# The modulation sums of two k-tiles move from TensorE to VectorE

## The chip, the cores and the metric

The kernel runs on one core of one Trainium2 chip. The metric is the device time of one execution in microseconds (us). The kernel before takes 2005.23 us, the median of three runs (2004.79 to 2006.36). Traces come from the hardware profiler, which records one execution.

## The reference, cut to what matters

One trunk layer of a diffusion backbone works on 384 tokens of width 2048: 128 context tokens and 256 latent ones. All arithmetic is fp32.

```
m = silu(cond) @ w_mod + b_mod        # (2048) @ (2048, 6*2048), once per condition
sh1, sc1, g1, sh2, sc2, g2 = split(m, 6)
h = rms_norm(x, n1) * (1 + sc1) + sh1 # context tokens take c_ctx's row, latent ones c's
p = h @ w_in                          # (384, 2048) @ (2048, 4096): q, k, v, u
... attention, Fourier mixing, gates, output projection, SwiGLU FFN
```

The change touches how `sh1` and `sc1` of norm 1 are made: two matrix-vector products over 2048 rows and 2 x 2048 columns, for two conditions. Each 128 of the 2048 channels of `h` are one k-tile of the product with `w_in`. A k-tile of `h` can be made only when its shift and scale columns are there.

## The kernel before, in words

**Large products.** A weight is kept as a high and a low half in a reduced fp32 form, and so is `h`; each product is three matmuls (lines 170, 171 and 176: high-high, low-high, high-low). Work is cut into units: two k-tiles of weights by 512 columns (one k-tile where a group's count is odd), for the three tiles of 128 tokens. `next_unit` goes ahead of each unit. It has the next unit's weights split (`split`, line 155 on ScalarE for the high half, line 156 on VectorE for the low half), then ticks every side job in `behind`, and asks SyncE for one more load of weights. There are four raw buffers and three for each half.

**Groups.** The product with `w_in` has eight chunks of 512 columns (`ORDER`). It doesn't run chunk by chunk over all 16 k-tiles, since these come one after another. It runs in `GROUPS`: k-tile 0 for all chunks, then k-tiles 1 and 2, then 3 to 6, then 7 to 15. That makes 8 units in the second group, 16 in the third, and 40 in the last. After a chunk in a group, VectorE adds the PSUM tiles to the chunk's sum in SBUF (line 783). In the second and third group the PSUM tiles come from the pool `mm` with four buffers, three to a chunk.

**Norm 1's modulation.** `MODS` lists the k-tiles whose sums are made together as (first, count). `mod_sums` (lines 427 to 446) runs 8 steps for each entry: two k-rows of `w_mod`, shift and scale, four matmuls that use four column groups of the array side by side (line 436), each `count` x 128 columns wide. The weights come in tiles `wm` with four buffers, loaded by SyncE (line 419), two k-rows at a time (four where the count is one). When a step has used up a tile, the next load is asked for. After the last step ScalarE copies the sums (line 444). `mod_cols` turns them by TensorE transposes, one per k-tile (line 452), and VectorE adds the biases (lines 458 to 460). `modulate` makes a k-tile of `h`: ScalarE lines 553 and 155, VectorE line 156.

**The order.** All of this is written out by hand. `prepare` is a generator which yields after each step: a step of sums, with a step of the k-tiles before it as follower. `Paced` runs a generator at a rate: every unit adds `rate` to what is due, and when at least `least` is due, whole steps are run until less than one is left. `DUE` and `PREP` give the start and the rate in each group; in the last two groups `least` is 3.6, so that steps come in bursts. Thirteen steps are issued by hand in the opening. A unit whose k-tiles are not there forces steps (line 779).

**What follows.** When `prepare` ends, `with_rows` gives back the memory of `wm` and starts `rows`: the sums of the other four modulations. Those are made on VectorE (lines 361 and 363), from loads of 512 KB, summed over partitions by accumulating transfers on GpSimd's queue, and paced by `CHUNKS` in the last group. Before, counted from the rates, `prepare` ends in the fourth unit of the last group.

Of the kernel before, what the change touches and what calls it, by code (L numbers as in the profile page):

```python
# [13 lines left out]
F32 = mybir.dt.float32  # L14
F32R = mybir.dt.float32r
AF = mybir.ActivationFunctionType
ALU = mybir.AluOpType
AX = mybir.AxisListType

P = 128  # L20
D = 2048
KT = D // P
# [10 lines left out]
CH = 512  # L33
# [2 lines left out]
HALF = NL + NC  # L36


MODS = [(0, 1), (1, 2), (3, 2), (5, 2), (7, 3), (10, 3), (13, 3)]
GROUPS = [(0, 1), (1, 2), (3, 4), (7, 9)]  # L40
ORDER = [6, 7, 0, 1, 2, 3, 4, 5]
DUE = [-1.4, 0, 0, 0]
PREP = [1.75, 2.5, 1.8, 1.8]
PAIR = "t1 qk,,,,,lq,s0 s1 m0,e0,m1,i0 pv lb,e1,,i1 t0,,lv"


# [73 lines left out]
def trunk_kernel(ctx: ExitStack, tc: tile.TileContext, io: dict):  # L120
    nc = tc.nc
# [21 lines left out]
    dram = ctx.enter_context(tc.tile_pool(name="dram", bufs=1, space=DRAM))  # L143
# [90 lines left out]
    front, behind = [], []  # L234
# [25 lines left out]
    ident = consts.tile([P, P], F32, tag="ident", name="ident")  # L260
    make_identity(nc, ident)
    ones = consts.tile([P, 32], F32, tag="ones", name="ones")
    nc.vector.memset(ones, 1.0)
    csz = consts.tile([P, KT, 32], F32, tag="csz", name="csz")
# [8 lines left out]
    def new_h(kt):  # L273
# [16 lines left out]
    conds, ng, bcol = (first[:, 32 * i : 32 * i + 32] for i in range(3))  # L290
    ng = ng.rearrange("p (i k) -> p i k", i=2)
# [3 lines left out]
    ms1 = consts.tile([P, KT, 2, 2], F32, tag="ms1", name="ms1")  # L295
    msh, msc = (
        [ms1[:, :, i], consts.tile([P, KT, 2], F32, tag=f"ms2{i}", name=f"ms2{i}")] for i in range(2)
    )
# [8 lines left out]
    with ExitStack() as ph:  # L307
# [159 lines left out]
        with ExitStack() as pha:  # L467
            wmp = phm.enter_context(tc.tile_pool(name="wmp", bufs=4, side="right"))
            cpool = pha.enter_context(tc.tile_pool(name="cpool", bufs=12))
            tmp = pha.enter_context(tc.tile_pool(name="tmpa", bufs=2))  # L470
# [24 lines left out]
            def head_constants():  # L495
                nc.sync.dma_start(heads, io["heads"])
                yield
                yield
                yield
                nc.vector.tensor_scalar_mul(qg8, qg[:, 0:1], HD**-0.5)  # L500
# [42 lines left out]
            scales = Paced(scale())  # L543
# [12 lines left out]
            for t in range(NT):  # L556
                for cc in range(4):
                    turn(t, cc, acc_tile)
                    square(t, cc)
                    if t == 0 and cc == 2:  # L560
                        nc.scalar.activation(
                            out=csz[:, :, 0:2], in_=conds.rearrange("p (k c) -> p k c", c=2), func=AF.Silu
# [17 lines left out]
            prepared = [1]  # L580
# [13 lines left out]
            def prepare():  # L594

                follow = iter(())
                for k0, n in MODS[1:]:
                    for i, _ in enumerate(mod_sums(src, k0, n, wme, sums)):
                        if i:
                            next(follow, None)  # L600
                        yield
                    follow = columns_and_tokens(k0, n)
                    if k0 + n == KT:
                        prep.due = min(prep.due, 0)
                        yield
                    while k0 + n in (3, 7) and prepared[0] < k0 + n:
                        prep.due = min(prep.due, 0)
                        yield
                        while prepared[0] < k0 + n:
                            yield next(follow)  # L610
                for _ in follow:
                    yield

            prep = Paced(prepare())

            h0H, h0L = new_h(0)
            f0 = tmp.tile([P, TOK], F32, tag="hf", name="hf0")
# [110 lines left out]
                rpool = phr.enter_context(tc.tile_pool(name="rpool", bufs=1, side="right"))  # L728
                behind.append(rows)

            prep.then = with_rows
            behind += [scales, prep]

            def after(ci):
                a = acc[ci]
# [30 lines left out]
            for gi, (k0, n) in list(enumerate(GROUPS))[1:]:  # L766
                prep.due, prep.rate = DUE[gi], PREP[gi]
                prep.least = 3.6 if gi > 1 else 1
                if gi == len(GROUPS) - 1:
                    behind.append(Paced(head_constants(), 0.2))  # L770
                    new_ring()
                for rate, ci in zip(CHUNKS, ORDER):
                    if gi == len(GROUPS) - 1:
                        rows.rate = rate
                    po = [(mm_tile if gi < len(GROUPS) - 1 else acc_tile)() for _ in range(NT)]
                    for u in range(k0, k0 + n, 2):
                        w = next_unit()
                        while prepared[0] < min(u + 2, k0 + n):
                            prep.step()

                        def done(t):
                            a = acc[ci][:, t]
                            nc.vector.tensor_add(a, a, po[t])  # L783

                        unit(po, hH, hL, w, u, min(k0 + n - u, 2), u == k0, u + 2 >= k0 + n, done)
                    if gi == len(GROUPS) - 1:
                        behind.append(Paced(after(ci)))
# [407 lines left out]
    tmp = ctx.enter_context(tc.tile_pool(name="tmpx", bufs=2))  # L1195
# [207 lines left out]
    parts = [([], []) for _ in FF_PARTS]  # L1403
# [147 lines left out]
def _laid_out(inp):  # L1551


    def by_chunk(w):
        k, n = w.shape
        return w.reshape(k // P, P, n // CH, CH).transpose(2, 1, 0, 3)

    def columns(v):
        return v.reshape(-1, P).T

    out = _tables()
    for name in ("w_in", "w_na_proj", "w_fnet_proj", "w_gate", "w_o", "w_gate_up", "w_down"):
        out[name] = by_chunk(inp[name][0])
    x = np.concatenate([inp["x_prompt"][0], inp["x_sample"][0]], axis=0)
    out["x_in"] = x.reshape(NT, P, 4, CH).transpose(2, 1, 0, 3)

    w_mod, b_mod = inp["w_mod"][0], inp["b_mod"][0]
    shift_scale = w_mod[:, : 2 * D].reshape(KT, P, 2, D).transpose(1, 0, 2, 3)
    for kt0, n in MODS:
        out[f"w_mod{kt0}"] = shift_scale[..., kt0 * P : (kt0 + n) * P]  # L1570
    out["w_rows"] = w_mod[:, 2 * D :]
    out["b_mod"] = b_mod
    conds = np.stack([columns(inp["c_ctx"]), columns(inp["c"][0])], axis=2).reshape(P, -1)
    out["first"] = np.concatenate(
        [conds, columns(inp["norm1_g"][0]), columns(inp["norm2_g"][0]), columns(b_mod[: 2 * D])], axis=1
    )
    qg, kg = inp["q_norm_g"][0], inp["k_norm_g"][0]
    out["heads"] = np.concatenate(
        [np.tile(qg, 2)[:, None], np.tile(kg, 2)[:, None], np.tile(kg, (P, 1))], axis=1
    )  # L1580

    cache_k = inp["cache_k"][0, 0].reshape(P, NH // 2, P)
    out["cache_k"] = cache_k.transpose(1, 2, 0)
    out["cache_v"] = inp["cache_v"]

    q, c = np.arange(HD)[:, None], np.arange(HD)[None, :]
    h, rr, e = np.arange(NH), np.arange(2), np.arange(6)
    at = (
        h.reshape(8, 1, 1, 2, 1, 1) * 465
        + (5 + e.reshape(1, 1, 1, 1, 6, 1) - rr.reshape(1, 2, 1, 1, 1, 1)) * 31  # L1590
        + (15 + np.clip(c - q, -15, 15)).reshape(1, 1, HD, 1, 1, HD)
    )
    w0 = np.clip(q - 8, 0, 48)
    inside = ((c >= w0) & (c < w0 + 16)).reshape(1, 1, HD, 1, 1, HD)
    places = np.append(inp["rpb"][0].reshape(-1), np.float32(-1e30))
    out["rpb"] = places[np.where(inside, at, len(places) - 1)].reshape(8, P, 2, 6, HD)
    return {n: np.ascontiguousarray(a) for n, a in out.items()}
# [27 lines left out]
```

## Time and profile before

| what | value |
|---|---|
| median of three runs | 2005.23 us |
| the profiled execution | 2005.29 us |
| its span, first to last instruction | 2003.5 us |
| TensorE busy | 1989.5 us (99%) |
| VectorE busy | 1226.0 us (61%) |
| ScalarE busy | 718.3 us (36%) |
| GpSimd busy | 73.9 us (4%) |
| line 436, the sums on TensorE | 448 records, 13.4 to 168.9 us |
| granted TensorE clock | 1.0 throughout |

In the rows of the profile PE is TensorE, PEld its weight loads, DVE VectorE, ACT ScalarE, POOL GpSimd, SP SyncE. A group row gives line, engine and operation, output and inputs, count, then busy time and mean ns of one, then the engine's idle time just before them and what ended it. A timeline row gives start and duration in us; a duration of several instructions run together is from the first start to the last end. In brackets stands the idle time before, and who ended it. A matmul of fp32 data leaves two records, a transpose one. Ends of matmuls are modelled, and some records are missing.

### The profile page before, as it was taken

Reading aid. Unit: us, or ns where it says so; the run is one execution under the profiler, and the core shown is the slowest. Engines: PE = TensorE matmul, PEld = TensorE weight load, DVE = VectorE, ACT = ScalarE, POOL = GpSimd, SP = SyncE. Lnnn points to the kernel's source line nnn. Section 1 sums busy time; section 2 is a strip of 40 time slices with the busy share of each in tenths; the row PEclk is TensorE's granted clock in tenths of the full one; section 3 lists DMA queues with packets and bytes.
Section 4 is the critical chain, followed back from the end, with each engine's and each line's share of the span. In section 5 each row is a group of like instructions: output and inputs, shape, how many; then the busy total and the mean of one; then the engine's idle time right before and its main releaser. Section 6 shows DMA issues by size and latency. Waiting matters only on the chain.

```text
span 2003.5 us, 24190 instructions
## 1 busy us (share of the span) xinstructions
PE 1989.5 (99%) x9404; PEld 1628.4 (81%) x9404; DVE 1226.0 (61%) x1493; ACT 718.3 (36%) x1052; POOL 73.9 (4%) x106
## 2 busy tenths in 40 slices
PE   8999999999999999999999999999999999999999
PEld 5767888887777888889988888888888888888887
DVE  6745999879877886776843454554334433434654
ACT  6324332445554443344423322323232233223231
POOL 0000010101010100100001000001000000000000
PEclk9999999999999999999999999999999999999999
DMA  9896898888886898764457464547444544455463
GB/s 347 289 342 206 308 288 312 271 278 283 269 255 216 284 330 264 252 231 131 134 182 200 158 189 164 188 139 211 137 150 129 165 153 131 132 152 174 158 185 104
DMA packets 140658, 425.28 MB, mean 212 GB/s; under 512 B 17856, under 2 KB 39296, under 8 KB 139520
## 3 DMA queue, kind: packets, MB, share of 16 engines
q1 hardware_dynamic: 127344, 400.51, 60.4%
q0 software_dynamic: 9600, 16.88, 3.9%
q10 hardware_dynamic: 3600, 6.34, 0.9%
q8 instruction: 74, 1.21, 0.2%
q14 instruction: 40, 0.33, 0.0%
HBM read 387.50 MB, written 44.63 MB: 216 GB/s over the span
## 4 chain that ended last, share of the span: by engine, by line
PE 95%; DMA 2%; DVE 2%; ACT 1%; issue 1%; SPq 0%; DVEq 0%; ACTq 0%
PE mm L170 19%; PE mm L176 18%; PE mm L171 18%; PE at L170 10%; PE at L171 10%; PE at L176 10%; PE at L436 1%; DMA wm<-in_w_mod 1%; PE at L1039 1%; PE at L977 1%; PE at L1056 1%; DVE wl L156 1%; PE at L1447 1%; PE at L1453 1%; PE mm L1453 1%; PE mm L1447 1%
## 5 line engine op out<-in xcount | busy, mean ns | idle before, releaser
L156 DVE TENSOR_TENSOR wl<-wraw,wh 128x1024 fp32r<-128x1024 f32 (+1 forms) x464 | 553.7, 1202 | 435.1 <-ACT wh L155 251.7
L155 ACT CAST wh<-wraw 128x1024 fp32r<-128x1024 f32 (+1 forms) x464 | 478.5, 1038 | 757.9 <-PE mm L171 454.1
L170 PE MATMUL mm<-wh,hH 128*128 128x512 f32 x1316 | 518.2, 394 | 0.3 <-ACT hH L155 0.3
L171 PE MATMUL mm<-wh,hL 128*128 128x512 f32 x1316 | 513.2, 390 | 0.2
L176 PE MATMUL mm<-wl,hH 128*128 128x512 f32 x1316 | 357.2, 389 | 0.2 <-DVE wl L156 0.2
L363 DVE SCALAR_TENSOR_TENSOR accr<-wmr,csz,accr 128x1024 f32<-128x1024 f32 x240 | 301.6, 1278 | 4.6 <-DMA wmr<-in_w_rows 4.6
L170 PEld LDWEIGHTS mm<-wh,hH 128*128 128x128 f32 x1316 | 247.0, 188 | 65.6 <-issue 12.7
L176 PEld LDWEIGHTS mm<-wl,hH 128*128 128x128 f32 x1316 | 246.9, 188 | 52.2 <-DVE wl L156 0.6
L171 PEld LDWEIGHTS mm<-wh,hL 128*128 128x128 f32 x1316 | 247.2, 188 | 50.6 <-DVE hL L156 0.8
L170 PE MATMUL at<-wh,hH 128*128 128x512 f32 x616 | 240.1, 390 | 0.0
L171 PE MATMUL at<-wh,hL 128*128 128x512 f32 x616 | 239.7, 389 | 0.0
L176 PE MATMUL at<-wl,hH 128*128 128x512 f32 x616 | 169.4, 389 | 0.0
L176 PEld LDWEIGHTS at<-wl,hH 128*128 128x128 f32 x616 | 115.6, 188 | 24.0
L171 PEld LDWEIGHTS at<-wh,hL 128*128 128x128 f32 x616 | 115.7, 188 | 23.9
L170 PEld LDWEIGHTS at<-wh,hH 128*128 128x128 f32 x616 | 115.6, 188 | 23.9
L170 PE MATMUL mm<-wh,cH 128*128 128x512 f32 x278 | 108.1, 389 | 0.0
L171 PE MATMUL mm<-wh,cL 128*128 128x512 f32 x278 | 108.1, 389 | 0.0
L176 PE MATMUL mm<-wl,cH 128*128 128x512 f32 x278 | 76.6, 389 | 0.0
L170 PE MATMUL at<-wh,cH 128*128 128x512 f32 x196 | 76.2, 389 | 0.0
L171 PE MATMUL at<-wh,cL 128*128 128x512 f32 x196 | 76.2, 389 | 0.0
L783 DVE TENSOR_TENSOR acc<-acc,mm 128x512 f32<-128x512 f32 x60 | 40.4, 685 | 43.8 <-PE mm L176 43.8
L171 PEld LDWEIGHTS mm<-wh,cL 128*128 128x128 f32 x278 | 52.2, 188 | 10.8
(287 smaller groups left out, 1817.1 us busy)
## 6 DMA issues: line engine op xcount, KB each, us to landing
wraw<-in_w_gate_up SPq DMA_DIRECT2D x176, 512.0 KB, 3.8
wmr<-in_w_rows SPq DMA_DIRECT2D x128, 512.0 KB, 5.2
wraw<-in_w_down SPq DMA_DIRECT2D x88, 512.0 KB, 3.9
wraw<-in_w_gate SPq DMA_DIRECT2D x64, 512.0 KB, 5.0
wraw<-in_w_in SPq DMA_DIRECT2D x60, 512.0 KB, 5.6
wm<-in_w_mod SPq DMA_DIRECT2D x24, 768.0 KB, 6.1
wraw<-in_w_o SPq DMA_DIRECT2D x32, 512.0 KB, 6.2
wm<-in_w_mod SPq DMA_DIRECT2D x28, 512.0 KB, 6.1
```

What stands on the lines that cost most here:

```text
L155: nc.scalar.copy(H, x)
L156: nc.vector.tensor_sub(L, x, fr(H))
L170: nc.tensor.matmul(po[t], H[k0 + i][:, sl], wH[:, i], start=first and i == 0, stop=False)
L171: nc.tensor.matmul(po[t], L[k0 + i][:, sl], wH[:, i], start=False, stop=False)
L176: nc.tensor.matmul(po[t], H[k0 + i][:, sl], wL[:, i], start=False, stop=last and i == n - 1)
L363: nc.vector.scalar_tensor_tensor(out=acc[:, cnd], in0=wm, scalar=sc, in1=acc[:, cnd], op0=ALU.mult, op1=ALU.add)
L436: nc.tensor.matmul(pm[q : q + 32, :w], csz[:, k, :], wm[:, kk + par, ty, :], start=k < 2, stop=k >= KT - 2, tile_position=(0, q), skip_gro ...
L783: nc.vector.tensor_add(a, a, po[t])
L977: nc.tensor.matmul(po[j][:, cols], t["q"][rows[j], q], t["k"][rows[j], k], start=True, stop=True, tile_position=(j * HD, 0),)
L1039: nc.tensor.transpose(o[:, i * P : (i + 1) * P], sc[:, j, c0 : c0 + P], ident)
L1447: nc.tensor.matmul(o, a, xH, start=u + kk == 0, stop=False)
L1453: nc.tensor.matmul(o, a, wide(u + kk)[0], start=False, stop=last and kk == 1)
```

## The change

`MODS` ends with `(13, 1)` in place of `(13, 3)`; k-tiles 14 and 15 go to a new generator, `last_columns`. For each of the 16 k-rows it has GpSimd load one piece of 512 columns (shift and scale of two k-tiles, 256 KB) into one of two buffers, and VectorE multiplies it by the two conditions and adds it to two running sums (two operations of 128 x 512). The first two pieces are asked for in the first step, and piece k + 2 after the operations on piece k. Then two matmuls with a matrix of ones sum over the partitions, ScalarE copies the result, and GpSimd writes two rows to DRAM and reads them back as eight rows of 128. TensorE turns these, VectorE adds the biases, and the two k-tiles of `h` are made.

The generator is paced at 0.95 steps a unit from the second group on, and at 1 in the last group. The pace of `prepare` in the third group goes from 1.8 to 1.65 steps a unit, and its start from 0 to 0.3. What is left of `prepare` is run whole when the last group begins, and `rows` starts there.

```diff
-MODS = [(0, 1), (1, 2), (3, 2), (5, 2), (7, 3), (10, 3), (13, 3)]
+MODS = [(0, 1), (1, 2), (3, 2), (5, 2), (7, 3), (10, 3), (13, 1)]
+LAST = (14, 2)
-DUE = [-1.4, 0, 0, 0]
-PREP = [1.75, 2.5, 1.8, 1.8]
+DUE = [-1.4, 0, 0.3, 0]
+PREP = [1.75, 2.5, 1.65, 1.8]
...
-                    if k0 + n == KT:
+                    if (k0, n) == MODS[-1]:
                         prep.due = min(prep.due, 0)
                         yield
...
+            def last_columns():
+                kt0, n = LAST
+                some, parts_n = slice(kt0, kt0 + n), 4 * n * P // CH
+                total = tmp.tile([P, 2, 2 * n * P], F32, tag="total", bufs=1, name="total")
+                def load(k):
+                    wm = tmp.tile([P, 2 * n * P], F32, tag="wml", bufs=2, name=nm("wml"))
+                    nc.gpsimd.dma_start(wm, io[f"w_mod{kt0}"][:, k].rearrange("p i n -> p (i n)"))
+                    return wm
+                got = [load(0), load(1)]
+                yield
+                for k in range(KT):
+                    wm = got[k]
+                    for cnd in range(2):
+                        a, sc = total[:, cnd], csz[:, k, cnd : cnd + 1]
+                        if k == 0:
+                            nc.vector.tensor_scalar_mul(a, wm, sc)
+                        else:
+                            nc.vector.scalar_tensor_tensor(
+                                out=a, in0=wm, scalar=sc, in1=a, op0=ALU.mult, op1=ALU.add
+                            )
+                    if k < KT - 2:
+                        got.append(load(k + 2))
+                    yield
+                o = at_tile()
+                parts = total.rearrange("p c n -> p (c n)")
+                for g in range(parts_n):
+                    nc.tensor.matmul(
+                        o[32 * g : 32 * g + 32], ones, parts[:, g * CH : (g + 1) * CH], start=True, stop=True,
+                        tile_position=(0, 32 * g), skip_group_check=True,
+                    )
+                row = tmp.tile([P, CH], F32, tag="junk", bufs=1, name=nm("lrow"))
+                nc.scalar.copy(row[: 32 * parts_n], o[: 32 * parts_n])
+                for g in range(parts_n):
+                    nc.gpsimd.dma_start(s_last[g : g + 1], row[32 * g : 32 * g + 1])
+                yield
+                yield
+                r = tmp.tile([P, 2 * n * P], F32, tag="wml", bufs=2, name=nm("lcol"))
+                nc.gpsimd.dma_start(r[: 4 * n, :P], s_last.rearrange("g (q p) -> (g q) p", p=P))
+                yield
+                yield
+                o = at_tile()
+                nc.tensor.transpose(o[:, : 4 * n], r[: 4 * n, :P], ident[: 4 * n, : 4 * n])
...
+            last = Paced(last_columns(), 0.95)
+            def prepare_step():
+                (prep if prep.live else last).step()
...
-            prep.then = with_rows
-            behind += [scales, prep]
+            behind += [scales, prep, last]
...
                 if gi == len(GROUPS) - 1:
+                    prep.drain()
+                    with_rows()
+                    last.rate = 1
...
-                            prep.step()
+                            prepare_step()
```

More of the change, by code (lines that the diff above doesn't have):

```diff
@@ L614, in trunk_kernel @@
             prep = Paced(prepare())
+            s_last = dram.tile([4 * LAST[1] * P // CH, CH], F32, tag="last", name="s_last")
+            def last_columns():
[40 more added lines that the diff above has]
+                nc.tensor.transpose(o[:, : 4 * n], r[: 4 * n, :P], ident[: 4 * n, : 4 * n])
+                m = o[:, : 4 * n].rearrange("p (c i k) -> p k i c", c=2, i=2)
+                yield
+                while prepared[0] < kt0:
+                    prep.step()
+                b = bcol.rearrange("p (i k) -> p k i", i=2)[:, some].unsqueeze(3).to_broadcast([P, n, 2, 2])
+                nc.vector.tensor_add(ms1[:, some], m, b)
+                nc.vector.scalar_tensor_tensor(
+                    out=msc[0][:, some], in0=msc[0][:, some], scalar=1.0,
+                    in1=ng[:, 0, some].unsqueeze(2).to_broadcast([P, n, 2]), op0=ALU.add, op1=ALU.mult,
+                )
+                yield
+                for kt in range(kt0, KT):
+                    modulate(kt)
+                    prepared[0] = kt + 1
+                    yield
@@ L1568, in _laid_out @@
     shift_scale = w_mod[:, : 2 * D].reshape(KT, P, 2, D).transpose(1, 0, 2, 3)
-    for kt0, n in MODS:
+    for kt0, n in MODS + [LAST]:
         out[f"w_mod{kt0}"] = shift_scale[..., kt0 * P : (kt0 + n) * P]
```

## The prediction

> **What bounds the kernel now.** I read the engine totals first, then stage by stage, then the waits of TensorE.
>
> ```profile
> PE 1989.5 (99%) x9404; PEld 1628.4 (81%) x9404; DVE 1226.0 (61%) x1493; ACT 718.3 (36%) x1052; POOL 73.9 (4%) x106
> ```
> ```profile
> 0.00:57.00 57.00, 49.83 (x354) 33.05 (x354) 35.45 (x67) 32.89 (x66) 0.69 (x6) 1.00 0.92 338
> 57.00:173.50 116.50, 115.96 (x678) 81.78 (x679) 64.70 (x97) 37.81 (x57) 0.00 (x0) 1.00 0.82 298
> 173.50:340.00 166.50, 166.50 (x737) 137.89 (x736) 151.66 (x167) 54.71 (x64) 9.26 (x12) 1.00 0.86 289
> 340.00:2003.50 1663.50, 1657.23 (x7637) 1375.67 (x7636) 974.15 (x1165) 592.85 (x866) 63.98 (x88) 1.00 0.61 194
> ```
> ```profile
> PE at L511 <- DMA xc<-in_x_in: 3.8, 1, 3.8
> PE at L436 <- DMA wm<-in_w_mod: 3.1, 5, 0.7
> ```
>
> The columns of the stages are length, busy time of TensorE, its weight loads, VectorE, ScalarE and GpSimd, clock, DMA share, GB/s. From 57 us on TensorE is busy for all but 0.5 us until 173.5, and without a pause until 340. Only the opening waits, and there the DMA engines are the limit (0.92). So TensorE work taken out after 57 us is worth its own length, and each new wait of TensorE costs its own length: nothing later gives it back. The profiled execution took 2005.29 us (span 2003.5), 0.06 us off the median of the three runs; the sum is made against 2005.29.
>
> **What is removed from TensorE.** The sums of k-tiles 13 to 15 are eight steps, of 384 columns each; they become eight steps of 128.
>
> ```profile
> 17.14 0.64 PE L436 MATMUL at<-wm,csz 128*32 128x128 f32 x16
> 123.48 1.50 PE L436 MATMUL at<-wm,csz 128*32 128x384 f32 x16
> 124.91 0.55 PE L452 MATMUL at<-ident,mrow 128*128 128x128 f32 x3
> 125.39 1.50 PE L436 MATMUL at<-wm,csz 128*32 128x384 f32 x16
> 135.22 2.79 PE L436 MATMUL at<-wm,csz 128*32 128x384 f32 x32
> 168.53 0.85 PE L436 MATMUL at<-wm,csz 128*32 128x384 f32 x8
> ```
>
> Eight records are one step. From 8 to 32 records the time grows by 2.79 - 0.85 = 1.94 us, so a step of 384 columns costs 0.65 us and a burst 0.20 us of tail besides. At 128 columns two steps take 0.64: less that tail, 0.22 each. Saved: 8 x 0.43 = 3.4 us. Three transposes hold TensorE for 0.48 (124.91 to 125.39); two of them go, 0.3 us.
>
> **What is added to TensorE.** Two products with the ones, 512 columns each, in two column groups. A step above is two passes over 384 columns in four groups at once, 0.325 us a pass; two passes over 512 columns are 0.87 if the two groups run at once, 1.74 if one after the other. L436 shows groups running at once, so I take 0.9. The transpose of eight rows lies between 0.05 and 0.3 (a whole one: 0.16); I take 0.15. Balance on TensorE: -3.4 - 0.3 + 0.9 + 0.15 = **-2.65 us**.
>
> **New waits.** I counted by hand which step each unit of work issues (one tick per unit, rates 2.5, 1.65, 0.95).
>
> (a) The opening. The first two pieces depend on nothing, and GpSimd, which issues them, has nothing to do after its constants. So they start beside the first loads: 2 x 256 KB more.
>
> ```profile
> 13.40 0.65 PE L436 MATMUL at<-wm,csz 128*32 128x128 f32 x16 [0.65 <-DMA wm<-in_w_mod]
> 14.58 0.64 PE L436 MATMUL at<-wm,csz 128*32 128x128 f32 x16 [0.53 <-DMA wm<-in_w_mod]
> 15.86 0.64 PE L436 MATMUL at<-wm,csz 128*32 128x128 f32 x16 [0.64 <-DMA wm<-in_w_mod]
> 14.00:15.00 1.00, 0.47 (x20) 0.38 (x16) 0.20 (x2) 0.72 (x2) 0.00 (x0) 1.00 1.01 410
> ```
>
> TensorE waits for each 512 KB of weights in turn, at 1.18 and 1.28 us apart, with the DMA engines full (1.01). Another 512 KB ahead of them moves all of it by about 1.25 us. Bounds: 0, if they fell into a gap, and 1.3; I take **+1.25**, as no gap is seen there. [...] No row of before has GpSimd loading in the opening, so the trace alone doesn't settle it.
>
> (b) VectorE at the end of the group of two k-tiles. Each piece is two operations of 512 columns.
>
> ```profile
> L363 DVE SCALAR_TENSOR_TENSOR accr<-wmr,csz,accr 128x1024 f32<-128x1024 f32 x240 | 301.6, 1278 | 4.6 <-DMA wmr<-in_w_rows 4.6
> 200.19 2.48 DVE L363 SCALAR_TENSOR_TENSOR accr<-wmr,csz,accr 128x1024 f32<-128x1024 f32 x2
> L783 DVE TENSOR_TENSOR acc<-acc,mm 128x512 f32<-128x512 f32 x60 | 40.4, 685 | 43.8 <-PE mm L176 43.8
> 73.28:87.11 13.83, 13.83 (x85) 10.04 (x84) 11.42 (x20) 5.17 (x8) 0.00 (x0) 1.00 0.90 339
> 87.11 1.28 DVE L783 TENSOR_TENSOR acc<-acc,mm 128x512 f32<-128x512 f32 x2
> 88.56 0.39 PE L170 MATMUL mm<-wh,hH 128*128 128x512 f32 x1
> 89.47 0.39 PE L170 MATMUL mm<-wh,hH 128*128 128x512 f32 x1
> ```
>
> Back to back an operation of 1024 columns takes 1.20 us; one of 512 columns between 0.60 (half of it) and 0.69 (the add of 512), so 1.3 a piece and 21 us for 16. They spread over the first 18 of 24 units, where VectorE is at 64.7 of 116.5 us, so nearly all hides. Not at one place: from 73.28 to 87.11 VectorE has 13.83 - 11.42 = 2.41 us idle, and four pieces want 5.2. The add at 87.11 comes 2.8 us late and ends at 90.6. The product at 89.47 writes the buffer of the second next tile (four buffers, three to a chunk), which that add must have read: **+1.1 us**. Bounds 0 and 1.8 (pieces of 1.48).
>
> (c) One burst outgrows the weight buffers. With the start 0.3 and 1.65 steps a unit, and steps held back until 3.6 are due, the group's ticks issue 3, 3 and 4 steps; then two ticks bring 3.5, which is not enough, and the third makes it 5.15: five steps at once. In before no burst has more than four. The five are `10:0` to `10:8` of the sums of k-tile 10, all of 384 columns, and there are four buffers of `wm`: the fifth's load can only be issued once the first step has run.
>
> ```profile
> 124.40 0.33 SPq L419 DMA_DIRECT2D wm<-in_w_mod  x1
> ...
> DMA to landing us min/median/max: 4.2/4.2/4.2
> DMA to landing us min/median/max: 3.6/6.1/9.3
> ```
>
> The burst of 123.48 has its first replacement issued 0.92 us after it began (124.40), landing 4.2 us later (second row; the third is over all 52 loads). So the fifth step's weights come 5.1 us after the burst began. TensorE gets there after four steps, their tail and three transposes: 4 x 0.65 + 0.1 + 0.48 = 3.2 us. **+2.0 us**; with 3.6 to landing 1.3, with the median 6.1 it is 3.8.
>
> (d) Two transposes lose the cover of ScalarE's copy, which they need. Ahead of the one for k-tiles 10 to 12 stood 1.3 us of sums; now it is two steps of 0.22. And tile 13's last step is drained together with its transpose when the last group begins, with nothing between.
>
> ```profile
> 17.86 0.27 ACT L444 COPY mrow<-at 128x128 f32<-128x128 f32 x1 [0.36 <-PE at L436]
> 18.27 0.27 PE L452 MATMUL at<-ident,mrow 128*128 128x128 f32 x1
> 138.07 0.48 ACT L444 COPY mrow<-at 128x384 f32<-128x384 f32 x1 [3.36 <-PE at L436]
> ```
>
> In the opening the sums end at 17.78 (17.14 + 0.64) and the transpose starts at 18.27: 0.49 us for a copy of 128 columns, 0.70 with one of 384. The first place has 0.44 of cover: **+0.3**. The second has none: **+0.5** (0.3 to 0.8 each way for both together, by how much of the tail counts).
>
> (e) The rows of the other modulations start with the last group's first unit instead of its fifth, so their VectorE work moves up by 4 x 1.95 steps of 1.20 us, 9.4 us. They share the head of the group with the last two k-tiles.
>
> ```profile
> 173.50:194.20 20.70, 20.70 (x94) 17.11 (x93) 11.29 (x16) 9.78 (x15) 0.00 (x0) 1.00 0.55 192
> 194.20:340.00 145.80, 145.80 (x645) 120.78 (x644) 140.38 (x152) 44.93 (x49) 9.26 (x12) 1.00 0.90 302
> 249.66 1.22 DVE L156 TENSOR_TENSOR wl<-wraw,wh 128x1024 fp32r<-128x1024 f32 x1
> 254.15 1.07 PE L176 MATMUL mm<-wl,hH 128*128 128x512 f32 x4
> ```
>
> Before the rows VectorE has 20.70 - 11.29 = 9.4 us idle: room for exactly that. But the first rows' weights can be asked for only after tile 13's transpose, and land 4.2 us later, so part of that room is gone; I put VectorE some 2.6 us later behind TensorE than before. From 194 us it is 96% busy and can't catch up. The low half made at 249.66 is done at 250.9 and wanted at 254.15, a reserve of 3.3 us, the smallest I saw there. So this is hidden, barely: I take **+0.3**, between 0 and 3.
>
> Hidden for certain are the small transfers through GpSimd's queue (two pieces ahead are two units, over 8 us, against 4.2 to land; nothing else stands in that queue before 258 us) and the last two k-tiles, ready at the third unit and wanted at the fourth and fifth. If a piece came late, VectorE would stand with the next low halves behind it.
>
> **Sum:** -2.65 + 1.25 + 1.1 + 2.0 + 0.8 + 0.3 = +2.8, so 2005.29 + 2.8 = **2008.1 us**. With every bound at its low end it is -2.65 + 1.3 + 0.3 = -1.05 (2004.2); at its high end, -1.75 + 1.3 + 1.8 + 3.8 + 1.1 + 3.0 = +9.2 (2014.5).
>
> **Rivals.**
>
> *The clean gain.* The loads of the opening slip into unused moments, the boundary and the long burst cost nothing; -2.65 + 0.8 gives 2003.4, and with the copies covered too 2002.6. For it: VectorE, the DMA engines and GpSimd have idle time on the mean. Against it: each of the three places named is one without it. It needs the fifth load to land within 2.3 us, which none of 52 did (least 3.6).
>
> *The queue of VectorE becomes the bound.* Place: the last group's first five chunks. Point: once VectorE is over 3.3 us later than before, a low half comes after TensorE wants it. What is over is then lost, and lost again where the rows' sums go out and VectorE waits for the buffer: a lag of 5 to 6 us costs 2 to 3 us once or twice, 2008.1 + 4 = 2012. For it: 96% busy. Against it: my lag of 2.6 stays under 3.3, and after one boundary between rows there are two empty steps.
>
> *Pieces come late.* The change doesn't fetch ahead: a piece lands more than 8 us after it was asked for. Speaking for it is the landing of 9.3 us at most in this stage. Four such pieces at 1.3 us late each, two of them beyond VectorE's slack: +2.6, 2010.7. Against: pieces of 256 KB are a third of those that took 6.1.
>
> **How the numbers follow.** My forecast 0.60, the clean gain 0.18, VectorE's queue 0.14, late pieces 0.08. The forecast's own range, with (a) to (e) varied one or two at a time, is 2005.5 to 2010.5. Some 0.2% (4.0 us) is what a measurement tells here: faster is below 2001.2, slower above 2009.2. The forecast lies 0.33 beyond the upper line and not below the lower one; with the queue (0.13) and the late pieces (0.05) beyond it too, slower is 0.38. Faster asks for the clean gain and 1.4 us more from the rows' earlier start: 0.08. The rest, 0.54, is no change. The range reaches to the clean gain below and to the queue above: 2002.6 to 2012.
>
> **What would show it.** After 57 us TensorE's sums have 64 records fewer of 384 columns and 64 more of 128. (a): the bursts of 13.40, 14.58 and 15.86 lie 1.2 us later, and so does the first large product. (b): a wait of TensorE for the add at the start of the group of four. (c): a wait of TensorE for `wm`, near 2 us, in one burst of five steps, which I place near 125 us. (d): TensorE waits for ScalarE's copy twice. (e): no wait for low halves in the last group. I am wrong if (a) or (c) is missing, or if a wait stands after 200 us.

## The result, and the profile after

The changed kernel is slower: 2020.3 us, the median of six runs (2018.35 to 2023.73), against 2005.8 us for the kernel before in the same comparison (six runs, 2004.79 to 2008.22). The ratio is 1.0073, with a 95% interval of 1.0062 to 1.0084; that is 14.6 us. Forecast were 2008.1 us, with a range of 2002.6 to 2012.0, so the result lies outside the range and on its slow side.

The profiled execution took 2022.65 us with a span of 2020.8, which is 2.35 us above the median of its runs; sums over this trace come out by about that much too large. First the page's engine totals, then the stages, with the columns that the prediction explains.

```profile
PE 1992.9 (99%) x9407; PEld 1630.7 (81%) x9407; DVE 1246.6 (62%) x1527; ACT 718.5 (36%) x1053; POOL 83.8 (4%) x125
```
```profile
0.00:57.00 57.00, 47.98 (x340) 32.34 (x341) 34.09 (x64) 31.84 (x65) 1.99 (x8) 1.00 0.92 334
57.00:173.50 116.50, 110.78 (x663) 78.25 (x662) 81.94 (x124) 33.48 (x48) 9.04 (x17) 0.99 0.82 294
173.50:340.00 166.50, 164.69 (x727) 134.14 (x726) 155.03 (x175) 56.95 (x71) 9.73 (x13) 1.00 0.84 280
340.00:460.00 120.00, 113.82 (x552) 95.66 (x551) 94.62 (x120) 47.91 (x84) 11.26 (x15) 0.97 0.86 278
```

Before, TensorE was busy for 115.96 of the second stage's 116.5 us and for all of the third. Now 5.7 us of the second are idle, 1.8 of the third, and 6.2 of a stage that reaches into the attention. In the second and the fourth the granted clock is no longer 1.00. TensorE's total rose by 3.4 us although it has less to do; in part that is since the same matmuls take longer at a lower clock (a step of 384 columns 1.51 us at 0.50, 0.85 at 1.00). TensorE's waits say what it stood for (total, times, longest):

```profile
PE at L512 <- DMA xc<-in_x_in: 5.6, 2, 3.8
PE at L437 <- DMA wm<-in_w_mod: 5.0, 5, 2.8
PE at L1110 <- DVE sc L1097: 4.7, 1, 4.7
PE at L162 <- DVE uL L157: 1.5, 1, 1.5
PE mm L172 <- DVE hL L157: 1.5, 1, 1.5
PE mm L177 <- DVE wl L157: 1.1, 3, 0.5
...
PE mm L171 <- DVE acc L854: 0.8, 1, 0.8
```

**Where the time went.** The weights of the large products are loaded into TensorE in the same order in both kernels. The start of one load after, less the start of the same load before, is how far TensorE has fallen behind by then. I call it the lag, and all tables of lags here are worked out that way from two traces.

| at (us, trace of before) | lag | what lies in between |
|---|---|---|
| 58 | +2.05 | the opening |
| 94 | +4.98 | the boundary after the group of two k-tiles |
| 178 | +7.2 | TensorE work saved, the five-step burst, the transposes |
| 238 | +7.3 | nothing |
| 372 to 421 | +11.7 | waits for low halves in the last group, 255 to 365 us |
| 464 | +16.6 | one place in the attention |
| end | +17.1 | |

*The opening.* The issue queue of SyncE, after, then before (start, length, what is issued):

```profile
0.74 8.69 SPq L485 DMA_DIRECT2D xc<-in_x_in  x12
```
```profile
0.74 5.94 SPq L484 DMA_DIRECT2D xc<-in_x_in  x12
```

And GpSimd, after:

```profile
1.46 1.30 POOL L627 DMA_DIRECT2D wml<-in_w_mod  x2 [0.16 <-issue]
```

The pieces' loads do start with the first loads, as forecast. But SyncE also needs 2.75 us longer to issue its own twelve.

*The boundary.* TensorE's timeline shows two waits there, not one; VectorE's shows what the second is for:

```profile
92.54 0.50 PE L171 MATMUL mm<-wh,hH 128*128 128x512 f32 x1 [0.82 <-DVE acc L854]
98.73 0.50 PE L172 MATMUL mm<-wh,hL 128*128 128x512 f32 x1 [1.48 <-DVE hL L157]
```
```profile
95.20 1.41 DVE L639 SCALAR_TENSOR_TENSOR total<-wml,csz,total 128x512 f32<-128x512 f32 x2
96.52 1.22 DVE L157 TENSOR_TENSOR wl<-wraw,wh 128x1024 fp32r<-128x1024 f32 x1
98.13 1.02 DVE L157 TENSOR_TENSOR hL<-hf,hH 128x384 fp32r<-128x384 f32 x2
```

A piece (95.20) and a low half of weights stand ahead of the low halves of `h` (98.13) for which the next group's first products wait. The lag goes from 2.09 to 3.23 us at the first wait and to 4.98 at the second: a stop costs some 0.3 us more than its length here.

*The burst of five steps.* TensorE, the queue of SyncE, and the granted clock around it (the third value from the end, ahead of DMA share and GB/s):

```profile
132.56 1.50 PE L437 MATMUL at<-wm,csz 128*32 128x384 f32 x16
...
134.46 1.50 PE L437 MATMUL at<-wm,csz 128*32 128x384 f32 x16
138.78 1.51 PE L437 MATMUL at<-wm,csz 128*32 128x384 f32 x8 [2.82 <-DMA wm<-in_w_mod]
```
```profile
133.47 7.21 SPq L420 DMA_DIRECT2D wm<-in_w_mod  x5
```
```profile
138.00:138.50 0.50, 0.00 (x0) 0.00 (x0) 0.33 (x1) 0.50 (x2) 0.00 (x0) 0.91 1.06 442
...
139.00:140.00 1.00, 1.00 (x8) 0.00 (x0) 1.00 (x3) 0.08 (x1) 0.00 (x0) 0.50 1.01 418
...
141.50:142.00 0.50, 0.50 (x3) 0.36 (x3) 0.50 (x2) 0.00 (x0) 0.00 (x0) 0.68 1.06 442
```

The fifth step's load goes out 0.91 us after the burst began and TensorE stands for 2.82 us. Then a second cost follows: the clock falls to 0.50 at 138.41 (0.91 is 0.09 us at one half) and is full again at 141.82 (0.68). One step of 384 columns takes 1.51 us (138.78) where it took 0.85 before. From 138.78 on, 3.04 us at half rate are another 1.5 us of lag.

*The attention.* VectorE, GpSimd and TensorE:

```profile
441.30 0.76 DVE L362 TENSOR_SCALAR accr<-wmr,csz 128x1024 f32<-128x1024 f32 x1 [6.54 <-issue]
...
450.98 1.14 DVE L1097 TENSOR_SCALAR sc<-sc,sm 128x384 f32<-128x384 f32 x4
```
```profile
433.93 0.57 POOL L368 DMA_DIRECT2D s_sum<-accr  x1 [38.48 <-DVE accr L364]
441.50 0.90 POOL L374 DMA_DIRECT2D s_sum<-s_sum  x1 [7.00 <-DMA s_sum<-accr]
```
```profile
451.55 2.00 PE L1110 MATMUL at<-ident,sc 128*128 128x128 f32 x8 [4.67 <-DVE sc L1097]
```

A row's sum leaves its only buffer `accr` by a transfer issued at 433.93, for which GpSimd waits until 441.50. VectorE waits 6.54 us until it may begin the next sum, at 441.30; its row names no releaser, but the time is that of the transfer's end. The softmax stands behind that in its queue and ends late; TensorE waits 4.67 us for it, and its clock is at one half from 449.02 (0.48 us of the first stretch below) to 455.85:

```profile
449.00:449.50 0.50, 0.00 (x0) 0.00 (x0) 0.00 (x0) 0.50 (x1) 0.00 (x0) 0.52 0.99 369
...
455.50:456.00 0.50, 0.50 (x3) 0.42 (x2) 0.00 (x0) 0.00 (x0) 0.00 (x0) 0.65 0.98 123
```

In before the same boundary came after the softmax:

```profile
443.05 0.57 POOL L367 DMA_DIRECT2D s_sum<-accr  x1 [42.68 <-DVE accr L363]
```

### The profile page after: what moved, and what is told of

The parts are those of the page before. It is cut to its first block, busy times and chain, and to the rows that moved or that the text cites. A ratio compares the mean times of both kernels' runs of the same rounds, so it can differ in the third digit from the quotient of the medians.

```text
span 2020.8 us, 24311 instructions
## 1 busy us (share of the span) xinstructions
PE 1992.9 (99%) x9407; PEld 1630.7 (81%) x9407; DVE 1246.6 (62%) x1527; ACT 718.5 (36%) x1053; POOL 83.8 (4%) x125
## 4 chain that ended last, share of the span: by engine, by line
PE 90%; DVE 5%; DMA 2%; issue 1%; ACT 1%; SPq 0%; DVEq 0%
PE mm L171 18%; PE mm L172 17%; PE mm L177 17%; PE at L177 10%; PE at L171 10%; PE at L172 10%; DVE wl L157 2%; DVE accr L364 1%; DMA wm<-in_w_mod 1%; PE at L437 1%; DVE acc L854 1%; PE at L1048 1%; PE at L1110 1%; PE at L1127 1%; PE at L1524 1%
## 5 line engine op out<-in xcount | busy, mean ns | idle before, releaser
L171 PEld LDWEIGHTS mm<-wh,cH 128*128 128x128 f32 x278 | 52.2, 188 | 10.8
L177 PEld LDWEIGHTS mm<-wl,cH 128*128 128x128 f32 x278 | 52.2, 188 | 10.8
```

What stands on the lines that cost most here:

```text
L171: nc.tensor.matmul(po[t], H[k0 + i][:, sl], wH[:, i], start=first and i == 0, stop=False)
L177: nc.tensor.matmul(po[t], H[k0 + i][:, sl], wL[:, i], start=False, stop=last and i == n - 1)
```

## The experiments

Theory A is that the loss is a sum of waits at separate places, each of which goes when its own cause is taken away, and that the saving of TensorE work is real under them. Its rival B is that one common load is behind them (VectorE or the DMA engines are too full), so that taking one away moves the wait elsewhere. Each experiment takes out one piece. In the diffs, minus is the changed kernel where nothing else is said.

### The pace of the third group as it was

```diff
-DUE = [-1.4, 0, 0.3, 0]
-PREP = [1.75, 2.5, 1.65, 1.8]
+DUE = [-1.4, 0, 0, 0]
+PREP = [1.75, 2.5, 1.8, 1.8]
```

> The changed kernel with the third group's pace as before (start 0, 1.8 steps a unit), so that no burst of sums has over four steps. Theory A (the loss is a sum of separate waits, each with its own cause): the wait for wm in a five-step burst near 138 us goes, and with it the half clock that follows it; together about 4 to 5 us, so some 2015.5 us. Theory B (the added VectorE operations and transfers of the first 170 us are what costs, wherever they wait): the wait turns up elsewhere and the time stays within 1.5 us of the changed kernel.

Measured: 2017.92 us, ratio 1.0058 (1.0041 to 1.0075), between the two expectations; the interval overlaps the changed kernel's, so the trace has to decide. The longest wait for `wm` falls from 2.8 to 0.9 us and the clock stays full there:

```profile
130.00:140.00 10.00, 10.00 (x55) 7.20 (x53) 7.45 (x13) 6.32 (x11) 0.54 (x1) 1.00 1.01 403
```

The lag at 178 us is 2.5 instead of 7.2: in these two traces this one place costs 4.7 us, two thirds more than its stop. The wait in the attention stays, at 4.4.

### The rows started four units later

```diff
-                    with_rows()
...
+                        if (gi, ci, u) == (len(GROUPS) - 1, ORDER[0], 13):
+                            with_rows()
```

> The changed kernel with the rows of the other modulations started in the fourth unit of the last group, as before, instead of ahead of its first. Theory A: the waits for low halves from 255 to 365 us (5 us) and the wait of the attention's first probabilities near 447 us with its half clock (5.5 us) go, since the end of a row sum no longer falls on the attention's softmax: about 2010 us. Theory B: the delay after 173 us comes from what VectorE still owes from the first 173 us, and stays: about 2020 us.

Measured: 2014.58 us, ratio 1.0038 (1.0025 to 1.0051), the largest gain of the single steps, about halfway between the two expectations. The lag is 6.41 from 190 to 351 us without a change, 7.5 at 372 to 439, and 9.2 at the end; the longest wait in the attention is 0.8. Both the waits for low halves up to 365 us and the one in the attention came from the rows' earlier start. Not all of it is gained: behind 190 us 2.8 us are still lost, at other places (the longest a wait of 1.3 us for a low half at 376 us).

### The first two pieces held back

```diff
+                    if k < 2:
+                        nc.vector.memset(wm[:, :1], 0.0)
```

> The changed kernel with its first two pieces held back: VectorE writes one column of each buffer when their step comes, so the two loads start near 50 us and not at 1.5 us. Theory A: the opening is 2.25 us shorter (first large product near 19.7 instead of 22.1 us) and so is the whole, about 2018 us. Rival: the loads then fall on the weights wanted at 57 us, and 1.3 us come back there: 2019.3 us.

Measured: 2017.95 us, ratio 1.0062 (1.0047 to 1.0077). The time is theory A's, but the interval holds the rival's 2019.3 too; the trace speaks for A. SyncE's twelve loads are issued in 6.11 us again, and the lag at 45 us is 0.3 instead of 2.25, at 58 us -0.6.

```profile
0.74 6.11 SPq L485 DMA_DIRECT2D xc<-in_x_in  x12
```

### Only the two loads, in the kernel before

```diff
+            for k in range(2):
+                piece = tmp.tile([P, CH], F32, tag="wml", bufs=2, name=nm("wml"))
+                nc.gpsimd.dma_start(piece, w_rows[k * P : (k + 1) * P, 0:CH])
```

> The kernel before, with two transfers of 256 KB that nobody reads asked for by GpSimd at its start. Theory A: these alone make the opening 2.25 us longer: 2008.0 us. By the bytes alone, as predicted, 1.25 us: 2007.0 us. If the opening's delay came from something else in the change: 2005.8 us.

Measured: 2008.77 us, ratio 1.0015 (1.0006 to 1.0024). The lag is 1.52 at 45 us and 1.5 until 351 us: two unread loads cost this, with no other part of the change there, and nothing gives it back. The times alone (1.2 to 4.8 us by the interval) don't tell 1.25 from 2.25, and the profiled execution, 2007.25 us, is next to the fastest of ten. The issue of SyncE's loads lengthens here too:

```profile
0.74 8.34 SPq L484 DMA_DIRECT2D xc<-in_x_in  x12
```

### All three undone

The three edits of the first three experiments together, so that what is left is the move itself.

> The changed kernel with three parts undone at once: the third group's pace, the start of the rows and the hold on the first two pieces. Theory A (separate waits that add up): against before, 0.3 us of opening, 2.9 us where the second group ends, -2.65 us of TensorE work less, 0.5 us for the transpose at the last group's start, and about 2.8 us of later small waits as they stood with the rows undone: +2 to +4, 2009 us. Theory B (the parts share one cause, VectorE's load): the waits move to other places and it stays above 2012 us.

Measured: 2007.63 us, ratio 1.0008 (0.9999 to 1.0016). By their ratios, against the 14.6 us, undoing the parts one at a time gained 3.0, 7.0 and 2.2 us, 12.2 in sum; together they gain 13.0. Within their intervals (some 3 us each) they add up, as A says. What is left in the trace is the boundary, which none of the three touches (+2.9 us there: lag 0.49 at 85 us, 3.39 at 94), and the saving behind it (1.05 at 178).

### All three undone, and the pieces begun in the third group

```diff
-            last = Paced(last_columns(), 0.95)
+            last = Paced(last_columns(), 1.375, 8)
```

> The one before this, with the pieces begun in the third group (1.375 steps a unit there) and none in the second, where VectorE has four adds' worth of idle time less than they want. Theory A: the 2.9 us where the second group ends go, about 2005 to 2006 us, level with the kernel before or just under. Rival: two pieces in one unit outrun their loads, VectorE waits, and 1 to 2 us come back: 2007 us.

Measured: 2006.96 us, ratio 1.0008 (0.9999 to 1.0017), not told apart from the run before it. The time is what the rival expected. In its trace the waits of the boundary are gone (lag -1.2 at 94 us), and another has come, where two pieces stand ahead of a chunk's adds and the second of them is late: VectorE waits 3.52 us for its load:

```profile
PE mm L171 <- DVE acc L857: 1.9, 1, 1.9
```
```profile
119.22 1.42 DVE L641 SCALAR_TENSOR_TENSOR total<-wml,csz,total 128x512 f32<-128x512 f32 x2 [3.52 <-DMA wml<-in_w_mod]
```

The lag reaches +1.2 at 127 us and is -1.25 from 178 to 351 us.

### All three undone, without the pieces

Against the version with all three undone:

```diff
-                got = [load(0), load(1)]
...
-                    wm = got[k]
-                    for cnd in range(2):
...
-                    if k < KT - 2:
-                        got.append(load(k + 2))
+                    if k == 0:
+                        nc.vector.memset(total, 0.0)
```

> Pace and rows undone, and the sixteen pieces left out: neither their loads nor their multiply-adds are done (the sums of k-tiles 14 and 15 are set to zero), all else stays. It measures what TensorE alone wins. By the prediction's sum -2.65 + 0.5 us: 2003.6 us. If less is won on TensorE than counted, it lies at 2005.8.

Measured: 2003.87 us, ratio 0.9988 (0.9979 to 0.9997): 2.4 us faster (0.6 to 4.2). The lag goes from 0.35 at 127 us to -1.95 at 178 us, so TensorE's saving is 2.3 us. That is what there is to gain if the added work hides whole; none of the complete versions here beats the kernel before.

### Does a stop of TensorE halve its clock, and from which length on?

Two versions of the kernel before with one forced wait, in the second unit of the third group's sixth chunk. The long one has `range(11)` in place of `range(1)`.

```diff
+                            d = tmp.tile([P, CH], F32, tag="junk", bufs=1, name=nm("late"))
+                            nc.vector.tensor_copy(d, acc[ci][:, NT - 1])
+                            for _ in range(1):
+                                nc.vector.tensor_scalar_mul(d, d, 1.0)
+                            pause = at_tile()
+                            nc.tensor.transpose(pause[:, :P], d[:, :P], ident)
```

> The kernel before, with one forced wait of TensorE: after the sixth chunk of the third group VectorE copies the chunk's last sum and multiplies it once by 1.0 (512 columns each), and TensorE must transpose 128 columns of that before it goes on. The chunk's add took 0.69 us in the profile of before, and each of the two operations takes at most as much, so TensorE should stand still for 1.5 to 2.1 us. Theory (the granted clock is halved only after a stop of more than about 2.1 us, as in the two stops of the changed kernel where it fell): the clock stays 1.00, and the lag behind before that remains is the length of the stop and no more, 1.5 to 2.1 us. Rival 1 (any stop at this place halves the clock): granted clock near 0.5 for some 3 us after the stop, lag 3 us or more. Rival 2 (the half clock in the changed kernel had another cause than the stop): the same as the theory here, told apart by the run with the long wait.

> The kernel before with the same forced wait, but eleven multiplications by 1.0 instead of one: by the same bounds TensorE should stand still for some 4 to 9 us. Theory (a stop of more than about 2.1 us halves the granted clock): the clock falls to 0.50 some 2.1 to 2.3 us after the stop began and is back at 1.00 some 2.8 to 4.0 us after TensorE resumed; matmuls of 512 columns come at 0.45 us instead of 0.23 in that time, so that the lag is the stop plus 1.4 to 2.0 us. Rival (the half clock in the changed kernel had another cause): clock 1.00 throughout, lag equal to the stop.

Measured in one execution each. TensorE's wait in the short and in the long version:

```profile
PE at L792 <- DVE late L790: 1.8, 1, 1.8
```
```profile
159.31 0.45 PE L792 MATMUL at<-ident,late 128*128 128x128 f32 x1 [6.41 <-DVE late L790]
```

The clock in the short version, then in the long one:

```profile
155.00:156.00 1.00, 0.65 (x4) 0.59 (x5) 1.00 (x2) 0.97 (x4) 0.00 (x0) 1.00 0.92 377
```
```profile
155.00:156.00 1.00, 0.00 (x0) 0.00 (x0) 0.90 (x4) 0.97 (x3) 0.00 (x0) 0.80 0.26 100
...
161.00:162.00 1.00, 1.00 (x4) 0.81 (x3) 1.00 (x3) 0.06 (x1) 0.00 (x0) 0.50 0.75 139
162.00:163.00 1.00, 1.00 (x5) 0.76 (x5) 0.37 (x1) 0.97 (x3) 0.00 (x0) 0.78 0.91 360
```

The short stop leaves the clock at 1.00 and adds 2.15 us of lag (0.14 to 2.29), 0.35 more than its 1.8, with the transpose in it. The long stop began at 152.90; the clock falls at 155.60 (0.80 is 0.4 us at one half), 2.7 us into it, and is full at 162.44, 3.1 us after TensorE resumed. The lag grows by 8.2 us (-0.52 to 7.69), 1.8 more than the stop of 6.41; less the 0.35 that the short one shows too, the clock cost 1.45. At the half clock the products of 512 columns come 0.43 us apart (160.41 to 160.84), at the full one 0.23. Nothing of the change is in these kernels, so the stop of 6.41 us alone brought the half clock. The expectation's 2.1 to 2.3 us was too narrow, though, and one short stop doesn't show from which length on; the last section has the other stops.

### The pieces at another phase

Against the version with the pieces begun in the third group:

```diff
-            last = Paced(last_columns(), 1.375, 8)
+            last = Paced(last_columns(), 1.5, 7)
```

> The changed kernel with all three parts undone (pace of prepare in the third group, start of the rows, loads held back) and the 16 pieces begun at the end of the second group, at 1.5 steps a unit, so that the units that end a chunk carry one piece and the others two; the run before it of this kind had 1.375 steps a unit from the third group on, two pieces ahead of some of the chunk's adds, and there TensorE waited 1.9 us once for the add. Theory A (each wait costs its own length and the saving of TensorE work is 2.3 us): the wait for the add near 127 us falls below 1 us, the lag from 190 us on is -1.3 to -2.3 us, and the ratio lies between 0.998 and 1.001, level with the version that leaves the pieces out or a little above. Theory B (VectorE's load in the third group costs time wherever it stands): the same wait appears at another boundary, lag 0 or more, ratio 1.001 or above.

Measured: 2020.07 us, ratio 1.0067 (1.0053 to 1.0081), nearly all of the loss again. Theory A's numbers failed here, and theory B's hold. The wait for an add that the version before had at 121 us is gone, but one of 1.2 us stands ahead of another chunk's add, at 137 us. Three more came: a wait of 2.5 us for the low half of `h` at the boundary again, one that I hadn't thought of, and one of 2.5 us for a low half of weights at 383 us, behind a row's load for which VectorE had waited 4.4 us. The last takes the lag from 11.5 to 15.4, though the rows start as late as in the kernel before:

```profile
95.85 0.58 PE L172 MATMUL mm<-wh,hL 128*128 128x512 f32 x1 [2.55 <-DVE hL L157]
...
153.38 2.48 PE L650 MATMUL at<-total,ones 128*32 128x512 f32 x4 [5.87 <-DVE total L641]
```
```profile
PE mm L177 <- DVE wl L157: 2.5, 1, 2.5
```

The product with the ones is issued one step after the last piece. At this rate it stands in TensorE's queue before the last pieces are added up. It takes 2.48 us instead of 1.03 (same product in the version at 1.375 steps a unit), and the next product of 512 columns, at 155.80, takes 0.80 instead of 0.39; behind the forced stop, at a clock of 0.50, the first one took 0.78. VectorE itself waits for the pieces there:

```profile
148.24 1.41 DVE L641 SCALAR_TENSOR_TENSOR total<-wml,csz,total 128x512 f32<-128x512 f32 x2 [2.32 <-DMA wml<-in_w_mod]
...
152.50 1.41 DVE L641 SCALAR_TENSOR_TENSOR total<-wml,csz,total 128x512 f32<-128x512 f32 x2
```

### The same without the later loads

To tell late transfers from a full VectorE: the instructions stay, 14 of the 16 loads go.

```diff
-                    wm = got[k]
+                    wm = got[k % 2]
...
-                    if k < KT - 2:
-                        got.append(load(k + 2))
```

> The run before it with 1.5 steps a unit, but only the first two of the 16 pieces are loaded; VectorE multiplies and adds these two eight times each (so the sums of k-tiles 14 and 15 are wrong, all else is the same). VectorE's work and the order of every instruction stay, 14 loads of 256 KB are gone. Theory A, in the form that run left it (with two pieces ahead each piece takes a load's landing of some 5 us and the load is asked for only after the multiply-adds two pieces before; at 1.5 steps a unit that chain is slower than the steps, and TensorE's product with the ones stands ready before the last piece is there): the wait of 5.9 us for the sums ahead of that product falls below 1.5 us, no half clock follows, and the lag from 190 us on falls from 11.5 to between 0 and 3 us; the wait of 2.5 us for the low half at 95.85 stays within 1 us of that, since the first two pieces are still waited for. Theory B (VectorE is too full in the third group): the wait ahead of that product stays at 4 us or more.

Measured: 2010.87 us, ratio 1.0020 (1.0011 to 1.0030).

```profile
PE at L648 <- DVE total L641: 2.7, 1, 2.7
PE mm L172 <- DVE hL L157: 2.0, 1, 2.0
```

The wait ahead of the product with the ones falls from 5.9 to 2.7 us, between the two expectations, and the lag from 190 us on is 7.5, not 0 to 3. Late transfers make 3.2 us of that wait, VectorE's queue the rest. So at 1.5 steps a unit neither theory holds alone. With two pieces ahead the loads limit the pace, and VectorE's other work does too. The stop at the boundary is again followed by half a clock, here only after TensorE had resumed (at 96.99):

```profile
98.00:99.00 1.00, 1.00 (x5) 0.74 (x4) 1.00 (x3) 0.00 (x0) 0.00 (x0) 0.71 0.85 305
...
101.00:102.00 1.00, 1.00 (x4) 0.75 (x4) 0.60 (x1) 0.00 (x0) 0.00 (x0) 0.58 0.00 0
```

## Why the prediction was wrong, step by step

**The TensorE work, -2.65 us, was nearly right.** Without the pieces the lag falls by 2.3 us at that place, and the ratio of 0.9988 says 2.4, in both with what (d) costs. The product with the ones took 1.05 us where 0.9 was taken.

**(a) The opening: right place, too small.** +1.25 with a bound of 1.3; measured +2.05 at 58 us, +1.5 from the two loads alone, and 1.9 on the mean of all traces (last section). The step that failed is the bound: bytes by throughput. That GpSimd's loads hold up SyncE's by their bytes was an estimate that no row of before showed; the runs showed the +1.5 of the two loads alone. GpSimd's loads also lengthened the issue of SyncE's own twelve, from 5.94 to 8.69 us. Taking just the loads away brings the lag at 45 us from 2.25 to 0.3.

**(b) The boundary: right place, one of two waits.** +1.1, bounds 0 to 1.8; measured +2.9. The wait for the add is there with 0.82 us and 1.14 of lag, as forecast. That the same lateness also reaches the low halves of `h`, 1.48 us and 1.75 of lag, wasn't looked for: the step asked which buffer the add holds and not what else stands behind it in VectorE's queue.

**(c) The burst of five: right mechanism, too small.** +2.0, bounds 1.3 to 3.8; its stop is 2.82 us, and 2.32 and 1.74 in the second and third experiment, which keep the burst. So the stop was priced well. The load was issued 0.91 us into the burst (forecast 0.92), landed some 1.1 us later than taken, and TensorE was there at 3.4 us (3.2). The term left out is the clock: 1.5 us more, so that the burst cost 4.3 to 4.7. After the opening, before has no stop of TensorE of over 0.83 us, and its clock is 1.00 until 2002 us, past its last product (1999.30), so nothing there pointed to it.

**(d) The transposes** were forecast at 0.8 us. The waits ahead of them are 0.16 for the copy and 0.39 for an add:

```profile
157.37 0.55 PE L453 MATMUL at<-ident,mrow 128*128 128x128 f32 x3 [0.16 <-ACT mrow L445]
...
180.96 0.33 PE L453 MATMUL at<-ident,mrow 128*128 128x128 f32 x1 [0.39 <-DVE acc L854]
```

**(e) The rows' earlier start is the step that failed.** "Hidden, barely", +0.3 and at most 3; measured +4.5 in the last group and +5.4 behind it, of which 4.9 in the attention. The comparison was a reserve of 3.3 us against a lag of VectorE of 2.6, both rough, where VectorE was 96% busy. The reserve didn't last: the low halves are late from 255 us on. And it stopped at the last group's end. Starting the rows four units earlier moves each boundary between two rows of sums by as much, and one of them now falls ahead of a softmax, where VectorE's 6.54 us for the single buffer can't hide. The rival "VectorE's queue becomes the bound" (0.14) names this mechanism, with "lost again where the rows' sums go out"; it priced it at 4 us where it cost 9.9. Starting the rows later, and nothing else, took both waits away; 2.8 us came back elsewhere, so that it gained 7.

In one line: (a) was set at 1.25 and came to 2.05, (b) 1.1 and 2.9, (c) and (d) together 2.8 and some 4.5, (e) 0.3 and 9.9; with the saving of 2.3 that is 17.1, the lag at the end. (a), (b), (c) and (e) lie above their upper bounds. The test named in advance, no wait after 200 us, was the one that fell. That the pieces come late was no part of this kernel's loss; the runs at 1.375 and at 1.5 steps a unit show it becoming one, with 3.5 and 2.3 us of waiting for one piece. The argument against it, that a piece is a third of a load that took 6.1 us, didn't hold: after's pieces took 5.8 us to land in the median.

What stays open: against the version without the pieces (0.9988), the complete versions (1.0008) lose 4 us. With all three parts undone, the boundary's 2.9 us account for most of that. With the pieces begun later the boundary's waits are gone from the trace and the late piece's 1.9 us stand there instead; its profiled execution ends no later than that of the version without pieces, but the medians still lie 3 us apart. Three of its twelve executions (2009.69, 2011.24 and 2013.68 us) had a mean clock of 0.998, the others 0.999 or 1.0; where these three were below the full clock, the profiled one (1.0) doesn't show. What else the twelve lose stays open.

## What to carry to other kernels

Where one engine is busy without a pause, an edit that saves it 2 us loses if it makes that engine wait once for more than that (here 2.3 us saved, and single waits of 2.82 and 4.67); follow what a late instruction delays in its own queue, all the way to the next buffer that only one transfer frees. When work is started earlier, list the places where it will stand later on (boundaries, single buffers) and look at what they now fall in front of. A "barely hidden" with two rough numbers is a coin toss, and should be priced so.

## What the runs showed of the hardware that I had not expected

**Behind some stops of TensorE the granted clock was one half, for 3.41 or 6.83 us.** Worked out from the windows' rows as above:

| where | stop of TensorE | length | clock at half | fall after the stop's start |
|---|---|---|---|---|
| after, burst | 135.96 to 138.78 | 2.82 us | 138.41 to 141.82: 3.41 us | 2.45 us |
| after, attention | 446.88 to 451.55 | 4.67 us | 449.02 to 455.85: 6.83 us | 2.14 us |
| before with the long stop | 152.90 to 159.31 | 6.41 us | 155.60 to 162.44: 6.84 us | 2.70 us |
| 1.5 steps a unit | 93.30 to 95.85 | 2.55 us | 96.14 to 99.56: 3.42 us | 2.84 us |
| the same without the later loads | 94.96 to 96.99 | 2.03 us | 98.42 to 101.84: 3.42 us | 3.46 us |

The fourth row is from these:

```profile
96.00:97.00 1.00, 1.00 (x3) 0.76 (x4) 0.27 (x1) 0.00 (x0) 0.00 (x0) 0.57 1.04 432
...
99.00:100.00 1.00, 1.00 (x4) 0.80 (x4) 0.16 (x1) 0.00 (x0) 0.39 (x1) 0.72 0.32 119
```

In the last two rows the clock fell only after TensorE had resumed, 0.29 and 1.43 us later. The stop of 1.48 us (after, at 97.25) had no sequel: the clock is 1.00 from 96 to 104 us. Nor had the forced one of 1.8 us (1.00 from 145 to 168 us). The burst's stop of 1.74 us with the first two pieces held back probably had one: the mean clock between 57 and 173.5 us is 0.99 there, as in after, and 1.00 with the third group's pace as it was, where that stop is gone and those of the boundary stay. So these runs don't show a length that parts the stops with a half clock from those without, nor what sets the moment of the fall.

Nearly the same stop can cost more in one execution than in another: the one in the attention took 4.7 us in after and 4.4 and 4.2 in the first and the third experiment, and the mean clock between 340 and 460 us was 0.97 in after and 0.99 in the two others.

The price on top of a stop is, by my estimate, half of the time in which TensorE works at the half clock, as products of 512 columns come 0.43 us apart there instead of 0.23; that is at most 1.7 us for each 3.41 us at half. It was 1.5 at the burst and 1.45 at the forced stop.

**Two loads that GpSimd issued cost SyncE's more than their bytes.** 512 KB beside the first loads made SyncE's issue of twelve loads 8.69 us long instead of 5.94, and the opening later than the 1.25 us that the bytes by the throughput seen there give. One trace's opening scatters: in the eight other traces without such early loads the lag at 45 us lies between -0.34 and 0.61, in the four with them between 1.52 and 2.40. The means are 1.9 us apart. That the longer issue is what costs the rest is not shown.
